# The fp32 head of a rotary embedding: 32 partitions with all their positions in place of all partitions with four

## The chip, the cores and the metric

The kernel runs on one core of one Trainium2 chip. The metric is the device time of one execution in microseconds (us). Times before are the median of three runs, beside one more execution that was profiled.

## The reference

```python
# x: (8, 2048, 16, 64) float32; cos, sin: (2048, 32) float32
x1, x2 = x_pairs[..., 0], x_pairs[..., 1]     # neighbours in the last axis
out1 = x1 * cos - x2 * sin
out2 = x1 * sin + x2 * cos
out = stack([out1, out2], axis=-1)            # interleaved again, float32
```

The tables depend on the position alone, so they are the same for every batch and head. 67.1 MB are read and 67.1 MB written.

## The kernel before, in words

Partition p holds positions 16p to 16p+15 of every batch (`K` = 16 positions of `HD` = 1024 values each). One batch in bf16 is a row of `buf`, 32 KB in each partition; `buf` has `NX` = 5 rows, and `at[b]` says which row batch b uses: 4, 0, 1, 2, 3, 4, 0, 1. A batch in float32 is 64 KB for each partition, 8 MB in all.

Loads and stores (`load`, `store`, lines 57 and 60) are DMAs that convert between float32 in memory and bf16 in SBUF. They are issued by POOL into one software queue that runs in order. There are two DMAs outside this queue, which keep float32: the head, issued by ACT (line 95), and the last quarter of batch 7, issued by SP (line 136).

All arithmetic is on DVE, in place, three products or sums for each batch in `rotate`: `qt = x * s_tab` (L79), `x = x * c_tab` (L85), `x = x + swapped qt` (L91). `s_tab` and `c_tab` are bf16 tables that L104, L105 and L106 build from `sin_sb` and `cos_sb`.

The order is written out by hand. At the start, ACT issues the head: positions 0 to 3 of every partition of batch 0 (`HEAD` = 4) as float32, rows of 16 KB, into the tile `head` (named `st` in the profile). POOL issues the other twelve positions of batch 0, then cos, sin, batch 1 and batch 2, all without a wait. DVE casts the head into `buf` (L102), builds the tables, rotates batch 0 in two pieces (positions 0 to 3, then 4 to 15), and then rotates batch 1 with a gate: its L79 is cut in two after `GATE` = 14 positions, and between the parts DVE copies one element of batch 0's row onto itself:

```python
        for a, z in ((0, nk),) if gate is None else ((0, GATE), (GATE, nk)):
            ...
            if z < nk:
                one = buf[:1, at[gate], 0, :1]
                nc.vector.tensor_copy(out=one, in_=one)
```

The store of batch 0 has to wait for that copy (L84). Behind the store POOL issues the load of batches 3 and 4 (rows 2 and 3 of `buf`), and that of batch 5, which waits until batch 0 is stored. From there loads and stores alternate to the end.

Of the kernel before, what the change touches and what calls it, by code (L numbers as in the profile page):

```python
# [2 lines left out]

# [4 lines left out]


@with_exitstack  # L10
def kernel(
    ctx: ExitStack,
    tc: tile.TileContext,
    x: bass.AP,
    cos: bass.AP,
    sin: bass.AP,
    out: bass.AP,
):
    nc = tc.nc
    fp32 = mybir.dt.float32  # L20
    bf16 = mybir.dt.bfloat16
    mult = mybir.AluOpType.mult
    add = mybir.AluOpType.add

    B, S, H, D = x.shape
    P = 128
    K = S // P
    D2 = D // 2
    HD = H * D
    NX = 5  # L30
    HEAD = 4
    TAIL = 4
    GATE = 14

    x_t = x.rearrange("b (p k) h d -> p b k (h d)", p=P, k=K)
    out_t = out.rearrange("b (p k) h d -> p b k (h d)", p=P, k=K)
    cos_t = cos.rearrange("(p k) c -> p (k c)", p=P, k=K)
    sin_t = sin.rearrange("(p k) c -> p (k c)", p=P, k=K)

    consts = ctx.enter_context(tc.tile_pool(name="consts", bufs=1))  # L40
    rows_pool = ctx.enter_context(tc.tile_pool(name="rows", bufs=1))
    stage = ctx.enter_context(tc.tile_pool(name="stage", bufs=1))

    cos_sb = consts.tile([P, K * D2], fp32)
    sin_sb = consts.tile([P, K * D2], fp32)
    c_tab = consts.tile([P, K, D], bf16)
    s_tab = consts.tile([P, K, D], bf16)


    buf = rows_pool.tile([P, NX, K, HD], bf16, name="xt")  # L50
    at = [4, 0, 1, 2, 3, 4, 0, 1]

    def place(b, n=1, k0=0, k1=K):
        return buf[:, at[b] : at[b] + n, k0:k1]

    def load(b, n=1, k0=0, k1=K):
        nc.gpsimd.dma_start(out=place(b, n, k0, k1), in_=x_t[:, b : b + n, k0:k1])  # L57

    def store(b, n=1, k0=0, k1=K):
        nc.gpsimd.dma_start(out=out_t[:, b : b + n, k0:k1], in_=place(b, n, k0, k1))  # L60

    def rotate(b, k0=0, k1=K, gate=None, to=None):
        nk = k1 - k0
        xp = buf[:, at[b], k0:k1]
        qt = stage.tile([P, K, HD], bf16, name="qt", tag="work")

        def rows(a):
            return a.rearrange("p k (h e) -> p k h e", h=H, e=D)

        def tab(a, j0=0, j1=nk):  # L70
            return dataclasses.replace(
                a,
                offset=a.offset + (k0 + j0) * D,
                ap=[a.ap[0], [D, j1 - j0], [0, H], [1, D]],
            )


        for a, z in ((0, nk),) if gate is None else ((0, GATE), (GATE, nk)):
            nc.vector.tensor_tensor(  # L79
                out=rows(qt[:, a:z]), in0=rows(xp[:, a:z]), in1=tab(s_tab, a, z), op=mult  # L80
# [4 lines that stand above are left out]
        nc.vector.tensor_tensor(out=rows(xp), in0=rows(xp), in1=tab(c_tab), op=mult)  # L85
        q_swap = dataclasses.replace(
            qt, offset=qt.offset + 1, ap=[qt.ap[0], [2, nk * HD // 2], [-1, 2]]
        )
        x3 = xp.rearrange("p k (a j) -> p (k a) j", j=2)
        y3 = x3 if to is None else to.rearrange("p k (a j) -> p (k a) j", j=2)  # L90
        nc.vector.tensor_tensor(out=y3, in0=x3, in1=q_swap, op=add)  # L91

    with tc.manual_schedule():
        head = stage.tile([P, TAIL, HD], fp32, name="st", tag="work")
        nc.scalar.dma_start(out=head[:, :HEAD], in_=x_t[:, 0, :HEAD])
        load(0, k0=HEAD)
        nc.gpsimd.dma_start(out=cos_sb, in_=cos_t)  # L97
        nc.gpsimd.dma_start(out=sin_sb, in_=sin_t)  # L98
        load(1)
        load(2)  # L100

        nc.vector.tensor_copy(out=buf[:, at[0], :HEAD], in_=head[:, :HEAD])  # L102
        s2 = s_tab.rearrange("p k (i j) -> p (k i) j", j=2)
        nc.vector.tensor_copy(out=s2[:, :, 0], in_=sin_sb)  # L104
        nc.vector.tensor_scalar_mul(s2[:, :, 1], sin_sb, -1.0)  # L105
        nc.vector.tensor_copy(  # L106
            out=c_tab.rearrange("p k (i j) -> p (k i) j", j=2),
            in_=cos_sb.to_broadcast([P, K * D2, 2]),
        )

        rotate(0, 0, HEAD)
        rotate(0, HEAD, K)
        rotate(1, gate=0)
        store(0)
        load(3, 2)
        load(5)
        rotate(2)
        store(1, 2)
        rotate(3)
        store(3)  # L120
        load(6, 2)
        rotate(4)
        rotate(5)
        store(4, 2)
        rotate(6)
        store(6)
        rotate(7, 0, K - TAIL)
        store(7, k1=K - TAIL)

        tail = buf[:, at[3], : 2 * TAIL].rearrange("p k e -> p (k e)").bitcast(fp32)
        tail = tail.rearrange("p (k e) -> p k e", e=HD)
        nc.vector.tensor_copy(out=buf[:1, at[6], 0, :1], in_=buf[:1, at[7], K - 1, :1])  # L134
        rotate(7, K - TAIL, K, to=tail)
        nc.sync.dma_start(out=out_t[:, 7, K - TAIL :], in_=tail)


# [1 line left out]
_INS = ['x', 'cos', 'sin']  # L140
_OUTS = [((8, 2048, 16, 64), 'float32')]


# [23 lines left out]
```

## Time and profile before

| | |
|---|---|
| median of 3 runs | 316.08 us (316.03 to 316.14) |
| profiled execution | 316.17 us |
| its span in the trace | 314.4 us |
| DVE busy | 215.4 us (69%), 37 instructions |
| POOL busy | 8.6 us (3%), 18 instructions |
| memory read, written | 67.63 MB, 67.11 MB; 429 GB/s over the span |
| head: issue to landing | 14.5 us |
| sin: issue to landing | 21.4 us |

The span runs from the first to the last instruction in the profile; the execution's own time is 1.77 us longer. In the profile's slices each digit is the busy share of one fortieth of the span (7.86 us) in tenths. A line of an engine's groups gives busy us and mean ns, and behind the second bar the idle time just before the group and what ended it. In a chain or a timeline the first number is the start in us from the span's start and the second the duration. A line of waits gives us in total, times, longest. A line of DMA issues ends with KB each and us from issue to landing; KB are counted at the destination, so a casting load of 8 MB in memory counts 4096 KB. ACTq and POOLq are the sequencers of ACT and POOL that issue DMAs.

### The profile page before, as it was taken

What the parts mean: (1) busy time and instruction counts of PE and PEld (TensorE: products, weight loads), DVE (VectorE), ACT (ScalarE), POOL (GpSimd) and SP (SyncE); (2) the same over time, 40 slices, a digit from 0 to 9 for tenths busy, and PEclk for the clock granted to TensorE, in tenths of its full rate; (3) what the DMA queues carried; (4) which work ended last, traced back from release to release, by engine and by line L of the source; (5) the groups of instructions that cost most, each with busy time, mean ns of one, the idle gap of its engine ahead of it and who ended that gap; (6) DMA issues with size and microseconds to landing.
All of it is one profiled execution on the core that took longest, in us unless ns stands there. A gap on an engine that the chain in (4) does not pass through costs nothing.

```text
span 314.4 us, 113 instructions
## 1 busy us (share of the span) xinstructions
DVE 215.4 (69%) x37; POOL 8.6 (3%) x18
## 2 busy tenths in 40 slices
DVE  0029999999999206999999999300009999980550
POOL 3000000100000000000000000000000000000000
DMA  8999999999999999999999999999999999999996
GB/s 253 264 284 200 200 204 263 267 400 417 317 200 200 208 258 200 200 284 517 400 400 475 459 400 400 242 225 200 200 300 434 400 400 534 400 400 400 434 500 267
DMA packets 2688, 102.24 MB, mean 325 GB/s; under 512 B 256, under 2 KB 256, under 8 KB 384
## 3 DMA queue, kind: packets, MB, share of 16 engines
q0 software_dynamic: 2400, 98.04, 96.8%
q10 hardware_dynamic: 144, 2.10, 1.8%
q1 hardware_dynamic: 144, 2.10, 1.6%
HBM read 67.63 MB, written 67.11 MB: 429 GB/s over the span
## 4 chain that ended last, share of the span: by engine, by line
DVE 62%; another core or an unknown queue 17%; DMA 17%; issue 0%; POOL 0%; DVEq 0%; PEldq 0%
DVE xt L91 21%; DVE xt L85 20%; DVE qt L79 20%; DMA out_dram<-xt 10%; DMA sin_sb<-in_sin_dram 7%; POOL xt L57 0%; DVE c_tab L106 0%; POOL cos_sb L97 0%; DVE s_tab L104 0%; DVE s_tab L105 0%; DVE xt L134 0%; DVE xt L84 0%; DVEq L79 0%; PEldq L162 0%
## 5 line engine op out<-in xcount | busy, mean ns | idle before, releaser
L79 DVE TENSOR_TENSOR qt<-xt,s_tab 128x16384 bf16<-128x16384 bf16 (+4 forms) x11 | 69.9, 6360 | 53.7 <-DMA xt<-in_x_dram 53.5
L91 DVE TENSOR_TENSOR xt<-xt,qt 128x16384 bf16<-128x16384 bf16 (+3 forms) x10 | 72.0, 7198 | 0.3
L85 DVE TENSOR_TENSOR xt<-xt,c_tab 128x16384 bf16<-128x16384 bf16 (+2 forms) x10 | 69.9, 6986 | 0.3
L102 DVE CAST xt<-st 128x4096 bf16<-128x4096 f32 x1 | 2.3, 2295 | 15.2 <-DMA st<-in_x_dram 15.2
L60 POOL DMA_DIRECT2D out_dram<-xt x6 | 3.6, 604 | 221.0 <-DVE xt L91 165.3
L134 DVE COPY xt<-xt 1x1 bf16<-1x1 bf16 x1 | 0.1, 144 | 12.0 <-DMA out_dram<-xt 12.0
L57 POOL DMA_DIRECT2D xt<-in_x_dram x6 | 3.8, 635 | 53.1 <-DMA out_dram<-xt 52.3
L104 DVE CAST s_tab<-sin_sb 128x512 bf16<-128x512 f32 x1 | 0.5, 451 | 6.3 <-DMA sin_sb<-in_sin_dram 6.3
L106 DVE CAST c_tab<-cos_sb 128x1024 bf16<-128x1024 f32 x1 | 0.7, 682 | 0.0
L98 POOL DMA_DIRECT2D sin_sb<-in_sin_dram x1 | 0.6, 562 | 0.0
L97 POOL DMA_DIRECT2D cos_sb<-in_cos_dram x1 | 0.6, 554 | 0.0
L105 DVE TENSOR_SCALAR s_tab<-sin_sb 128x512 bf16<-128x512 f32 x1 | 0.4, 441 | 0.0
L84 DVE COPY xt<-xt 1x1 bf16<-1x1 bf16 x1 | 0.1, 136 | 0.0
L151 POOL MEMSET const-float32-0.0<- 128x1 f32 x1 | 0.1, 98 | 0.2 <-issue 0.2
L151 POOL MEMSET const-bfloat16-1.0<- 128x1 bf16 x1 | 0.1, 101 | 0.0
L151 POOL MEMSET const-float32-1.0<- 128x1 f32 x1 | 0.1, 98 | 0.0
L151 POOL MEMSET const-uint8-127<- 128x1 uint8 x1 | 0.1, 98 | 0.0
## 6 DMA issues: line engine op xcount, KB each, us to landing
xt<-in_x_dram POOLq DMA_DIRECT2D x2, 8192.0 KB, 58.7
xt<-in_x_dram POOLq DMA_DIRECT2D x3, 4096.0 KB, 57.4
out_dram<-xt POOLq DMA_DIRECT2D x1, 6144.0 KB, 26.2
xt<-in_x_dram POOLq DMA_DIRECT2D x1, 3072.0 KB, 21.2
st<-in_x_dram ACTq DMA_DIRECT2D x1, 2048.0 KB, 14.5
out_dram<-xt SPq DMA_DIRECT2D x1, 2048.0 KB, 10.2
cos_sb<-in_cos_dram POOLq DMA_DIRECT2D x1, 256.0 KB, 21.3
sin_sb<-in_sin_dram POOLq DMA_DIRECT2D x1, 256.0 KB, 21.4
```

What stands on the lines that cost most here:

```text
L57: nc.gpsimd.dma_start(out=place(b, n, k0, k1), in_=x_t[:, b : b + n, k0:k1])
L60: nc.gpsimd.dma_start(out=out_t[:, b : b + n, k0:k1], in_=place(b, n, k0, k1))
L79: nc.vector.tensor_tensor(out=rows(qt[:, a:z]), in0=rows(xp[:, a:z]), in1=tab(s_tab, a, z), op=mult)
L85: nc.vector.tensor_tensor(out=rows(xp), in0=rows(xp), in1=tab(c_tab), op=mult)
L91: nc.vector.tensor_tensor(out=y3, in0=x3, in1=q_swap, op=add)
L97: nc.gpsimd.dma_start(out=cos_sb, in_=cos_t)
L98: nc.gpsimd.dma_start(out=sin_sb, in_=sin_t)
L102: nc.vector.tensor_copy(out=buf[:, at[0], :HEAD], in_=head[:, :HEAD])
L104: nc.vector.tensor_copy(out=s2[:, :, 0], in_=sin_sb)
L105: nc.vector.tensor_scalar_mul(s2[:, :, 1], sin_sb, -1.0)
L106: nc.vector.tensor_copy(out=c_tab.rearrange("p k (i j) -> p (k i) j", j=2), in_=cos_sb.to_broadcast([P, K * D2, 2]),)
L151: nc = _bacc.Bacc("TRN2", target_bir_lowering=False, num_devices=1)
```

## The change

The head becomes all sixteen positions of partitions 0 to 31 of batch 0 (`PH` = 32): 32 rows of 64 KB, the same 2 MB. It lands as float32 in the places of batches 3 and 4 in `buf` (rows 2 and 3, which together hold 64 KB in each partition), not in a tile of its own. POOL's first load is partitions 32 to 127 of batch 0, with all sixteen positions. The cast is over 32 partitions of 16,384 elements. Batch 0 is rotated in one piece, and the gate in batch 1 comes after fifteen positions, not fourteen. Lines from L104 on stand two lines lower in the changed file (the tables are built by L106, L107 and L108).

```diff
-    HEAD = 4
+    PH = 32
     TAIL = 4
-    GATE = 14
+    GATE = 15
...
-        head = stage.tile([P, TAIL, HD], fp32, name="st", tag="work")
-        nc.scalar.dma_start(out=head[:, :HEAD], in_=x_t[:, 0, :HEAD])
-        load(0, k0=HEAD)
+        head = buf[:PH, at[3] : at[3] + 2].rearrange("p r k e -> p (r k e)").bitcast(fp32)
+        head = head.rearrange("p (k e) -> p k e", e=HD)
+        nc.scalar.dma_start(out=head, in_=x_t[:PH, 0])
+        nc.gpsimd.dma_start(out=buf[PH:, at[0]], in_=x_t[PH:, 0])
         nc.gpsimd.dma_start(out=cos_sb, in_=cos_t)
         nc.gpsimd.dma_start(out=sin_sb, in_=sin_t)
         load(1)
         load(2)
 
-        nc.vector.tensor_copy(out=buf[:, at[0], :HEAD], in_=head[:, :HEAD])
+        nc.vector.tensor_copy(out=buf[:PH, at[0]], in_=head)
...
-        rotate(0, 0, HEAD)
-        rotate(0, HEAD, K)
+        rotate(0)
         rotate(1, gate=0)
         store(0)
         load(3, 2)
```

In the changed program the load of batches 3 and 4 has a wait on the head's DMA, which it had not before.

## The prediction

> **What bounds the kernel now.** I read the page's slices first, to see which resource never rests, then its DMA parts.
>
> ```profile
> span 314.4 us, 113 instructions
> DVE  0029999999999206999999999300009999980550
> DMA  8999999999999999999999999999999999999996
> q0 software_dynamic: 2400, 98.04, 96.8%
> q10 hardware_dynamic: 144, 2.10, 1.8%
> ```
>
> VectorE (DVE) has holes in every part of the span; the sixteen DMA engines have none. The trace also records every single DMA packet. Added up, the engines idle 0.26 us each between the first packet (1.77 us after the span's start) and the last, so DMA time bounds the kernel. A microsecond of engine time that is lost is a microsecond at the end, and nothing that VectorE saves shows unless it feeds the queue earlier.
>
> Next, the chain of waits that ended last, near the start, and the waits, for what VectorE waits on there.
>
> ```profile
> 2.44 21.39 DMA sin_sb<-in_sin_dram
> 23.83 0.02 issue
> 23.85 0.45 DVE s_tab L104
> ...
> 51.88 7.63 DVE qt L79
> 59.50 0.05 DVE xt L84
> ```
>
> ```profile
> DVE xt L102 <- DMA st<-in_x_dram: 15.2, 1, 15.2
> DVE s_tab L104 <- DMA sin_sb<-in_sin_dram: 6.3, 1, 6.3
> ```
>
> The head (first row) lands at 15.24, is cast, and then VectorE sits 6.3 us until sin has come through the software queue behind the rest of batch 0. So the cast is off the path: sin at 23.85 starts everything. The timeline shows where the chain gets back to the queue.
>
> ```profile
> 59.42 0.14 DVE L84 COPY xt<-xt 1x1 bf16<-1x1 bf16 x1
> 59.48 1.20 DVE L79 TENSOR_TENSOR qt<-xt,s_tab 128x2048 bf16<-128x2048 bf16 x1
> 59.85 0.54 POOL L60 DMA_DIRECT2D out_dram<-xt  x1 [55.77 <-DVE xt L84]
> ```
>
> The gate copy (L84) releases store(0), and store(0)'s first packet starts at 61.74, in the packet records, just as the first engine ends load(2) at 61.59. The queue is refilled with 0.15 us of rest on two or three engines: no slack. If VectorE is late against the queue, the engines idle; if both move together, the rest of the kernel moves with them.
>
> Last, durations by shape, and the DMA issues with their time to landing.
>
> ```profile
> L79 DVE TENSOR_TENSOR qt<-xt,s_tab 128x14336 bf16<-128x14336 bf16 x1 | 7.6, 7626 | 0.0
> L102 DVE CAST xt<-st 128x4096 bf16<-128x4096 f32 x1 | 2.3, 2295 | 15.2 <-DMA st<-in_x_dram 15.2
> L104 DVE CAST s_tab<-sin_sb 128x512 bf16<-128x512 f32 x1 | 0.5, 451 | 6.3 <-DMA sin_sb<-in_sin_dram 6.3
> ```
>
> ```profile
> st<-in_x_dram ACTq DMA_DIRECT2D x1, 2048.0 KB, 14.5
> sin_sb<-in_sin_dram POOLq DMA_DIRECT2D x1, 256.0 KB, 21.4
> ```
>
> **The head on the engines.** Before, each engine carries eight head packets of 16 KB, 0.61 to 0.63 us each (the first, alone, 1.0 to 1.5): 8 x 0.618 = 4.94. The changed head is 32 rows of 64 KB, two for each of 16 engines. No packet here writes 64 KB into SBUF; a 64 KB store row takes 2.43. The lower end is therefore 2 x 2.43 = 4.86, which is 0.08 less than now. But every transfer of the trace reaches 128 partitions. The strongest write into SBUF is the old head, 16 engines x 16 KB in 0.611, that is 429 GB/s or 3.35 GB/s for each partition (the casting loads write half of that). The new head asks 32 partitions for the same 429 GB/s, 13.4 each, four times anything shown. If a partition takes no more than shown, a row lasts 4 x 2.43 = 9.7, and the head costs 19.4, 14.6 more than the lower end. No row decides between one and four, and neither end is nearer, so I take the geometric middle, two: 4.86 a row, 9.72 in all, **+4.78** against 4.94.
>
> [...]
>
> **The rest of batch 0.** Eight rows of 48 KB for each engine (1.828 each, 14.6) become six of 64 KB (2.43 each, 14.6): nothing. The tables and loads 1 and 2 behind it are the same, so sin lands at 23.85 + 4.8 = 28.65.
>
> **When the head lands, and the cast.** Packets of the two queues alternate one for one in the records, and the software queue has none until 5.3 us. With doubled rows: first row from 1.77, 0.5 of start-up, to 7.1; one software row to 9.55; second row to 14.4; one more software row, as the head's completion mark waited for one before too, to 16.85; landed at 17.2. The cast now covers 32 partitions and 16,384 elements each: 2.295 + 12,288 x 0.521 ns (slope of the 4,096 and 16,384 wide products, 2.29 and 8.69) = 8.70 against 2.30. It ends at 25.9, covered by the wait for sin by 2.75 us. With full-speed rows the head lands at 9.95, the cast ends at 18.65, and sin at 23.85 still covers it. POOL has issued its loads by 4.1 and waits for the gate, so nothing queues behind the cast but the table builds.
>
> **VectorE up to the gate.** From L79's start to the gate was 34.29. Rotation 0 in one piece is 3 x 8.727 = 26.18 (start to start in the timeline); the gate's first part grows by 1,024 elements, 7.54 to 8.07: 34.25, 0.04 less. It drops three instructions and gives this back to the later gate. Gate and end of load(2) both move by about 4.8, and their 0.15 us of rest stays. Load(3,2) now also waits for the head's place to be free: it stands behind store(0), some 40 us after the cast, so this costs nothing; in the worst case above, with the cast ending at 35.6, it still does.
>
> **Sum.** The profiled execution took 316.17: a span of 314.4 and 1.77 around it. 316.17 + 4.78 = 320.95, and 0.09 less against the median of 316.08: **320.9**.
>
> **Rivals.**
>
> *Partitions don't matter.* The engines run at 26.8 GB/s each whether they read or write SBUF, so the limit seen is the engine's. Then the head costs 4.86, the cast is covered, and the time is 316.08 - 0.08 = 316.0. Against it: nothing shows that 32 partitions take what 128 took.
>
> *Faster.* The first 16 head packets take 1.0 to 1.5, not 0.61, so about 0.6 us is lost at the start. If long rows start at full speed, 0.6 + 0.08 = 0.68 is won, 315.4. It decides only if the first row takes 2.5 us or less; I see no reason why longer packets should start sooner.
>
> *The cast ends up on the path.* If the queue cuts each row into 16 KB packets as now, three of the eight, and the completion mark, alternate with 64 KB software rows of 2.43 instead of 1.83. From 5.65, where the fifth packet ends: 3 x 3.05, then 2.43, then 0.35 is 17.6; the cast ends at 26.3, and sin, with full-speed packets, at 23.85: 2.45 late at the gate, 318.5. For it: every hardware packet here is 16 KB; against: those packets are whole rows, and software rows of 64 KB go as one.
>
> *Steeper.* With rows of 9.7 the head lands at 26.9, the cast ends at 35.6 before sin at 38.4, and the time is 316.08 + 14.5 = 330.6. Slow writes and short packets together would be about as bad.
>
> *Half the engines.* If the head goes to eight engines, four full-speed rows each, and the rest of batch 0 to all, these eight get two rows too many: +4.86, 320.9 too. Packet durations tell it apart: 2.43 instead of 4.86.
>
> **How the numbers follow.** About 0.2%, 0.63 us, is what a measurement of this kernel can tell from no change. Chances: slowed rows or half the engines 0.65, with factors of 1.5 to 2.5, thus 318.5 to 323.3; no cost 0.20; cast on the path 0.06; steeper 0.06; faster 0.03. The likeliest gives 320.9. The range runs from 316.0, so that it holds the case without cost, to 322.8, which leaves out the steep case and the edge of the main one. Faster 0.03, the same 0.20, slower 0.77.
>
> **What would show it.** Right: hardware packets of 65,536 bytes that last near 4.9 us, the head landing near 17, sin near 28.6, the cast near 8.7 us and VectorE idle for some 2.7 between cast and tables, store(0) issued near 64.6, and everything later moved by the same 4.8. Wrong in the main term: head rows of 2.4, sin still at 23.85. Wrong in the cover: no idle before the table build, and DMA engines resting between load(2) and store(0).

## The result and the profile after

The changed kernel takes 321.10 us (median of 6 runs, 321.04 to 321.18), the kernel before 316.11 (6 runs, 316.00 to 316.23). The ratio is 1.0156, with a 95% interval of 1.0146 to 1.0166: slower by 4.99 us, where 4.8 was forecast. The profiled execution took 321.11, with a span of 319.3.

First the page of the changed kernel: its slices and its DMA queues.

```profile
span 319.3 us, 110 instructions
DVE  0094999999999602999999999500007999990560
DMA  9699999999999999999999999999999999999996
q0 software_dynamic: 2368, 98.04, 95.4%
q10 hardware_dynamic: 48, 2.10, 3.1%
```

The same 2.10 MB now take 3.1% of sixteen engines' span, 9.9 us, where they took 1.8%, 5.7 us. It is not because there are more packets: there are 48 instead of 144 (32 rows and 16 completion marks). The DMA row has no hole in which the extra time could disappear: its 6 is none, because a packet is counted in the slice where it starts, and the second head rows start in the first slice (6.2 to 7.3 us) and end in the second (11.3 to 12.4). Added up from the packet records, the engines idle 0.52 us each between the first packet and the last, where it was 0.26.

The waits of the changed kernel (total us, times, longest) and its chain of waits (start, us) show where it goes.

```profile
DVE xt L104 <- DMA xt<-in_x_dram: 15.7, 1, 15.7
DVE s_tab L106 <- DMA sin_sb<-in_sin_dram: 4.5, 1, 4.5
```

```profile
2.45 26.42 DMA sin_sb<-in_sin_dram
28.87 0.02 issue
28.89 0.04 DVE s_tab L106
```

Sin comes at 28.87 instead of 23.83. These 5.04 us are the whole slowdown. VectorE, now casting for 8.7 us after the head landed at 15.68, still sits 4.5 us before sin comes: the long cast is covered.

The groups by shape and the timeline show that VectorE did what was worked out for it.

```profile
L104 DVE CAST xt<-xt 32x16384 bf16<-32x16384 f32 x1 | 8.7, 8680 | 15.7 <-DMA xt<-in_x_dram 15.7
L79 DVE TENSOR_TENSOR qt<-xt,s_tab 128x15360 bf16<-128x15360 bf16 x1 | 8.2, 8159 | 0.0
```

```profile
64.42 0.14 DVE L84 COPY xt<-xt 1x1 bf16<-1x1 bf16 x1
64.48 0.67 DVE L79 TENSOR_TENSOR qt<-xt,s_tab 128x1024 bf16<-128x1024 bf16 x1
64.85 0.54 POOL L60 DMA_DIRECT2D out_dram<-xt  x1 [60.76 <-DVE xt L84]
```

Store(0) is issued at 64.85, 5.00 us later than before. Its first packets start at 66.45, in the packet records, 0.002 us after an engine has finished load(2); the 0.15 us of rest that was there before is gone. From there on everything is the old kernel, 5 us later. The DMA issues of the changed kernel end with the time to landing:

```profile
sin_sb<-in_sin_dram POOLq DMA_DIRECT2D x1, 256.0 KB, 26.4
...
xt<-in_x_dram ACTq DMA_DIRECT2D x1, 14.9
```

### The profile page after: what moved, and what is told of

Its sections match the earlier page's. It is cut to its first block, busy times and chain, and to the rows that moved or that the text cites. A ratio compares the mean times of both kernels' runs of the same rounds, so it can differ in the third digit from the quotient of the medians.

```text
span 319.3 us, 110 instructions
## 1 busy us (share of the span) xinstructions
DVE 221.3 (69%) x34; POOL 8.6 (3%) x18
## 4 chain that ended last, share of the span: by engine, by line
DVE 60%; DMA 18%; another core or an unknown queue 17%; issue 1%; POOL 0%; DVEq 0%; PEldq 0%
DVE xt L91 20%; DVE xt L85 20%; DVE qt L79 20%; DMA out_dram<-xt 10%; DMA sin_sb<-in_sin_dram 8%; POOL xt L98 0%; DVE c_tab L108 0%; POOL cos_sb L99 0%; DVE s_tab L107 0%; DVE xt L135 0%; DVE xt L84 0%; DVEq L79 0%; DVE s_tab L106 0%; PEldq L163 0%
## 5 line engine op out<-in xcount | busy, mean ns | idle before, releaser
L79 DVE TENSOR_TENSOR qt<-xt,s_tab 128x16384 bf16<-128x16384 bf16 (+4 forms) x10 | 69.8, 6981 | 54.2 <-DMA xt<-in_x_dram 54.0
L91 DVE TENSOR_TENSOR xt<-xt,qt 128x16384 bf16<-128x16384 bf16 (+2 forms) x9 | 71.8, 7981 | 0.3
L104 DVE CAST xt<-xt 32x16384 bf16<-32x16384 f32 x1 | 8.7, 8680 | 15.7 <-DMA xt<-in_x_dram 15.7
L106 DVE CAST s_tab<-sin_sb 128x512 bf16<-128x512 f32 x1 | 0.5, 456 | 4.5 <-DMA sin_sb<-in_sin_dram 4.5
L108 DVE CAST c_tab<-cos_sb 128x1024 bf16<-128x1024 f32 x1 | 0.7, 684 | 0.0
L107 DVE TENSOR_SCALAR s_tab<-sin_sb 128x512 bf16<-128x512 f32 x1 | 0.4, 443 | 0.0
## 6 DMA issues: line engine op xcount, KB each, us to landing
out_dram<-xt SPq DMA_DIRECT2D x1, 2048.0 KB, 10.2
```

Source lines behind the costliest of these rows:

```text
L79: nc.vector.tensor_tensor(out=rows(qt[:, a:z]), in0=rows(xp[:, a:z]), in1=tab(s_tab, a, z), op=mult)
L104: nc.vector.tensor_copy(out=buf[:PH, at[0]], in_=head)
L108: nc.vector.tensor_copy(out=c_tab.rearrange("p k (i j) -> p (k i) j", j=2), in_=cos_sb.to_broadcast([P, K * D2, 2]),)
```

## The experiments

The trace's packet records of the head decide most of these runs; their times are counted from the span's start. Here they are for all of them: median duration of a row by its place in the order, and the rate of sixteen engines at the last row's duration.

| kernel | head | bytes of a row | rows in order, us | GB/s | time, us |
|---|---|---|---|---|---|
| before | 0 to 127, 4 positions | 16 KB | 1.21, 0.61, 0.63, 0.62, 0.61, 0.62 x3 | 420 | 316.1 |
| changed | 0 to 31, 16 positions | 64 KB | 4.68, 5.12 | 205 | 321.1 |
| low64 | 0 to 63, 8 positions | 32 KB | 2.32, 2.56, 2.56, 2.28 | 230 | 320.9 |
| mid64 | 32 to 95, 8 positions | 32 KB | 1.88, 1.23, 1.23, 1.24 | 425 | 316.6 |
| half32 | 0 to 31, 8 positions | 32 KB | 2.30, 2.56 | 205 | 318.4 |
| quarter16 | 0 to 15, 16 positions | 64 KB | 8.39 | 125 | 322.5 |
| mid64_long | 32 to 95, 16 positions | 64 KB | 3.05, 2.42, 2.57, 2.62 | 400 | 327.4 |

The first row of a kernel differs from the next (1.21 against 0.61 in the kernel before, 4.68 against 5.12 in the changed one), and in low64 the last row, which follows a row of the other queue, took 2.28 after rows of 2.56; why was not tried. The middle rows are the clean ones.

**Which partitions.** Two kernels with the same head size and shape, 64 partitions with 32 KB each, differ in the partitions, and with them in the rows of `x` that are read, in the cast (two pieces in mid64) and in one more DMA for the rest of batch 0:

```diff
...
-        nc.scalar.dma_start(out=head, in_=x_t[:PH, 0])
-        nc.gpsimd.dma_start(out=buf[PH:, at[0]], in_=x_t[PH:, 0])
+        nc.scalar.dma_start(out=head, in_=x_t[0:64, 0, :HB])          # low64; HB = 8
+        nc.gpsimd.dma_start(out=buf[64:128, at[0], :HB], in_=x_t[64:128, 0, :HB])
+        load(0, k0=HB)
...
```

```diff
...
+        nc.scalar.dma_start(out=head, in_=x_t[32:96, 0, :HB])         # mid64
+        nc.gpsimd.dma_start(out=buf[0:32, at[0], :HB], in_=x_t[0:32, 0, :HB])
+        nc.gpsimd.dma_start(out=buf[96:128, at[0], :HB], in_=x_t[96:128, 0, :HB])
+        load(0, k0=HB)
...
+        nc.vector.tensor_copy(out=buf[32:64, at[0], :HB], in_=head[0:32])
+        nc.vector.tensor_copy(out=buf[64:96, at[0], :HB], in_=head[32:64])
```

> Head: 64 partitions (0 to 63), eight positions each, rows of 32 KB, the same 2 MB, float32; everything else of batch 0 by the software queue. Theories for the 5.12 us rows of the changed kernel: H (each half of the partitions, 0 to 63 and 64 to 127, takes at most what 0 to 31 took, 32 x 64 KB in two rows of 5.12 us, 205 GB/s): four rows of 2.56 us each, head 10.2 us of every engine, time 321.1 as in the changed kernel. Q (each quarter of 32 partitions takes at most 205 GB/s): two quarters, 410 GB/s, rows of 1.28 us, time 316.2. L (the length of 64 KB for one packet of the ACT queue is what is slow, wherever it goes): rows of 32 KB take 1.22 us, time 316.0.

Measured: 320.89, ratio 1.0144 (1.0129 to 1.0159), rows of 2.56.

> The same head of 64 partitions by eight positions, now partitions 32 to 95, cast in two pieces of 32 partitions; the software queue gets the rest of batch 0 in three DMAs. H: the head falls half on 0 to 63 and half on 64 to 127, 410 GB/s in all, so rows of 1.22 to 1.28 us and 316.0 to 316.4. Q: the same. L: the same. A shape that is slow merely because it has fewer than 128 partitions: 321 as in the run with partitions 0 to 63.

Measured: 316.62, ratio 1.0012 (1.0002 to 1.0021), rows of 1.23. DMA issues of low64, then of mid64:

```profile
xt<-in_x_dram ACTq DMA_DIRECT2D x1, 2048.0 KB, 15.0
...
sin_sb<-in_sin_dram POOLq DMA_DIRECT2D x1, 256.0 KB, 25.7
```

```profile
xt<-in_x_dram ACTq DMA_DIRECT2D x1, 2048.0 KB, 10.3
...
sin_sb<-in_sin_dram POOLq DMA_DIRECT2D x1, 256.0 KB, 21.0
```

The same 2 MB land 4.7 us sooner when the 64 partitions are 32 to 95, and sin comes 4.2 us sooner with them (at 24.43 instead of 28.61; its issue is 0.5 later in mid64). Twice the partitions brought nothing over 0 to 31 as long as they stayed in 0 to 63: rows of 32 KB in 2.56 us and rows of 64 KB in 5.12 are both 205 GB/s. So H holds here as far as 0 to 63, and Q falls; partitions 64 to 127 alone were not run. The 0.4 us that mid64 is above the kernel before goes with the head's first packet starting at 2.12 instead of 1.75; why it starts later was not tried.

**Half the bytes.** The same edit with partitions 0 to 31 and `HB` = 8, and the other 96 by the software queue.

> Head: partitions 0 to 31 with eight positions, rows of 32 KB, 1 MB instead of 2 MB. H and Q: two rows of 2.56 us for each engine, 5.1 instead of 2.4, half the loss of the changed kernel, time 318.6. L: rows of 1.22 us, 316.0. If something at the start other than the rows were lost (a fixed sum for a 32-partition transfer): 321.

Measured: 318.36, ratio 1.0064 (1.0047 to 1.0080), rows of 2.30 and 2.56; sin comes at 25.98, 2.15 later than in the kernel before; in the changed kernel it is 5.04 later. Half the bytes cost 2.2 us, just under half: the loss goes with the bytes and is no fixed sum.

**Fewer partitions.** `PH` = 16 in the changed kernel.

> The changed kernel with a head of 16 partitions (0 to 15), all sixteen positions, rows of 64 KB, 1 MB: one row for each engine. H (one limit of 205 GB/s for the whole half of 64 partitions): the row takes 5.12 us as in the changed kernel, 2.7 more than a full-speed row, time 318.7. [...]

Measured: 322.48, ratio 1.0200 (1.0184 to 1.0215), one row of 8.39 us for each engine, from 7.1 to 8.9. Half the bytes of the changed kernel cost more than all of them did there, 6.3 us against 5.0. So H's one common limit of 205 GB/s for partitions 0 to 63 is ruled out: 16 partitions ran at a lower rate than 32. It was not as low as half: half of 205 GB/s would be rows of 10.2 us, an estimate from the 5.12 of the changed kernel. The 16 rows start at 1.76 and the last ends at 11.2: 1 MB in 9.5 us is 110 GB/s. Five of the sixteen completion marks then take 3.0 to 3.3 us instead of 0.04, and the first software rows 2.7 to 3.9 instead of 2.43; why was not tried.

**Long packets.** 64 KB rows again, on partitions 32 to 95.

```diff
...
+        nc.scalar.dma_start(out=head, in_=x_t[32:96, 0])
+        nc.gpsimd.dma_start(out=buf[0:32, at[0]], in_=x_t[0:32, 0])
+        nc.gpsimd.dma_start(out=buf[96:128, at[0]], in_=x_t[96:128, 0])
...
+        nc.vector.tensor_copy(out=buf[32:64, at[0]], in_=head[0:32])
+        nc.vector.tensor_copy(out=buf[64:96, at[0]], in_=head[32:64])
```

> Head: partitions 32 to 95 with all sixteen positions, rows of 64 KB, 4 MB, cast in two pieces of 8.7 us; the rest of batch 0 in two DMAs of 32 partitions. [...] L (a 64 KB packet of the ACT queue is slow by itself): rows of 5.1 us. [...]

Measured: 327.38, ratio 1.0357 (1.0341 to 1.0372), rows of 2.42 to 2.62: a 64 KB packet is not slow by itself, L falls. Nor is it the reading: this kernel's software queue reads for partitions 0 to 31 the very rows that the changed head read, on sixteen engines at once, in 2.43 to 2.44 us each instead of 5.12; it writes them as bf16, 32 KB a row, which is 216 GB/s. The 11 us are lost in another way, seen in the DMA row, in the stretches of the trace (us, then busy DVE and POOL, clock, DMA share, GB/s) and in the waits of this kernel:

```profile
DMA  9999898509999898898999999989989999999998
```

```profile
60.00:63.00 3.00, 3.00 (x1) 0.00 (x0) 1.00 0.82 175
63.00:73.00 10.00, 9.93 (x5) 0.37 (x1) 1.00 0.00 0
73.00:76.00 3.00, 3.00 (x1) 0.88 (x2) 1.00 0.81 350
```

```profile
POOL out_dram L60 <- DVE xt L84: 68.1, 1, 68.1
DVE xt L105 <- DMA xt<-in_x_dram: 19.3, 1, 19.3
```

VectorE starts casting at 19.3 and has 17.4 us to do. There is no wait for sin any more, the gate comes 68.1 us after POOL is ready for it, and in the packet records no DMA engine moves a byte from 63.2 to 73.7. This is what a cast that ends up on the path looks like: holes in the DMA row, where the changed kernel has none.

**VectorE's part alone.** The kernel before, with `rotate(0)` in one piece and `GATE = 15`.

> The kernel before, with only the VectorE part of the change: batch 0 rotated in one piece and the gate after fifteen positions. All theories: gate 0.04 us earlier, end unchanged within 0.1 us, 316.1. If the split of batch 0 or the place of the gate mattered by itself: more than 0.3 us of difference.

Measured: 316.15, ratio 0.9998 (0.9988 to 1.0007). It is worth nothing that can be measured.

**The gate alone.** The changed kernel with `GATE = 14`.

> The changed kernel with the gate back at fourteen positions: store(0) issued 0.53 us earlier. If the queue is refilled just in time, it is still busy with load(2) then, and the time stays at 321.1. If the gate bound the end: 320.6.

Measured: 321.08, ratio 1.0156 (1.0139 to 1.0173). Its timeline has store(0) here:

```profile
64.20 0.54 POOL L60 DMA_DIRECT2D out_dram<-xt  x1 [60.11 <-DVE xt L84]
```

That is 0.65 earlier than in the changed kernel (0.53 from the gate, 0.12 because sin came that much sooner in this execution). Yet its first packet starts at 66.56, 0.002 us after an engine has finished load(2), and the end stays: the queue, not the gate, sets the pace.

## Why the prediction was right

**DMA time bounds the kernel, so lost engine time goes to the end one for one.** Right. Sin moved by 5.04, store(0) by 5.00, the time by 4.99.

**Head rows at twice the duration.** Right in size, 5.12 for the second row where 4.86 was taken, a factor of 2.1. The reason given was none: it was the geometric middle between two far ends, and that it fell on the measured size was luck. Neither end fits the runs. The lower one counts engines alone, 2.43 a row, and the upper one counts partitions alone, which low64 and mid64 refute: 64 partitions each, rows of 2.56 and of 1.23. What counts is which partitions: 0 to 63 together took the same 205 GB/s as 0 to 31. What lies behind that, no run shows.

**The sum of 4.78** came near by terms that partly cancel. From the packet records, for each engine: head 5.63 to 9.91, +4.28; it was sized +4.78. The old head was taken 0.69 too small, since its first packets, 1.21 and not 0.62, were left out of the 4.94, and the new one 0.19 too small. The first packet starts 0.13 later on the mean (1.87 to 2.00). The 4 KB packets of the tables went from 1.29 to 1.71, +0.43, and this term was missing. Its cause stays open: the engines reach the tables 1.00 us apart instead of 0.45, but in half32 they are 1.05 apart and the tables still take 1.29. Together that is 4.84 on the mean engine; the last one, for which the landing of sin waits, loses 5.00. (The packet times in the prediction, 1.77, 61.59 and 61.74, are 0.02 too late; nothing rests on it.)

**The rest of batch 0, no cost.** Right: 14.65 us for each engine, where it was 14.63.

**Landing of the head.** Wrong step, without consequence. A software row was put between the two head rows, as the queues alternate one for one before. The records show both head rows back to back (the second starts at 6.2 to 7.3, the first software row only at 11.3 to 12.4), although the software queue had moved its first row at 5.3 in the kernel before. So the head landed at 15.68 instead of 17.2, and the cover of the cast was 4.5 instead of 2.75. In low64 and mid64, three head rows go first, then the queues alternate. What decides when they begin to alternate was not tested.

**Cast, rotation and gate.** Right: 8.68 against 8.70; from the start of batch 0's L79 at 30.17 to the gate 34.25, as worked out; dve_only and gate14 confirm that neither end of the change in VectorE shows.

**The rivals.** No cost from fewer partitions: refuted, though 64 partitions, 32 to 95 in mid64, had rows of 1.23 and cost 0.4 us. Half the engines: refuted, as 32 rows of about 5 us lie on sixteen engines. Cast on the path: not here, and mid64_long shows its price, 11 us, when it is. Steeper: not with 32 partitions, but quarter16 has rows of 8.4. Faster: the first row did not take 2.5 us or less.

## What to carry to other kernels

When a transfer is moved to fewer partitions, ask which ones, not only how many: here 32 to 95 took 428 GB/s and 0 to 63 took 205, with the same bytes in rows of the same size. Ask also whether the DMA engines ever rest. Here they idled 0.52 us each, and the slow transfer was paid in full (sin 5.04 later, the end 4.99) though nobody waited for its data: the head landed 4.5 us before it had to, and the loss was in what stood behind it in the same engines. To see whether a late VectorE or slow packets cost the time, look for holes in the DMA row: here late work left them (mid64_long, no byte from 63.2 to 73.7 us), slow packets did not.

## What the runs showed of the hardware

- Sixteen engines wrote float32 rows at 205 GB/s into partitions 0 to 31 (changed kernel, rows of 64 KB in 5.12 us) and 0 to 63 (low64, rows of 32 KB in 2.56), at 428 GB/s into 32 to 95 (mid64, rows of 32 KB in 1.225), and at some 110 GB/s into 0 to 15 (quarter16, 1 MB in 9.5 us).
- The engines did no other queue's work beside the slow rows: the software rows of the changed kernel started at 11.3 to 12.4, each engine's when its second head row had ended.
- A row of 64 KB in memory went as one packet on the ACT queue (changed kernel, 32 packets of 65,536 bytes) as well as on the software queue (a 64 KB store row in 2.43 to 2.45 us).
- The head's first packet started at 1.73 to 1.76 us in the kernels whose head has 16, 32 or 128 partitions, and at 2.10 to 2.12 in the three with 64 partitions. The issue began at 0.74 or 0.75 in each, and took 0.36 to 0.37 us in the former and 0.52 to 0.59 in the latter; nothing here explains the rest.
